# An encoder's neighbourhood attention by pairs of heads: full-height score matmuls, outputs in alternating column halves, queries and keys split straight from PSUM

## The chip, the cores and the metric

The kernel runs on one core of a Trainium2 chip. A core has five engines with queues of their own: TensorE (PE in the profile, its weight loads PEld), VectorE (DVE), ScalarE (ACT), GpSimd (POOL) and SyncE (SP, which here only issues DMAs). The metric is the device time of one execution in microseconds, as the median of several runs. The profile is one further execution, recorded by the hardware profiler; its instructions carry the line numbers of the kernel's file.

## The reference

An encoder of two layers works on 1280 tokens of 1024 channels: 256 of a "prompt" (4 rows of 64) and 1024 of a "sample" (16 rows of 64), each attending only within itself. Layer 0 mixes tokens with a bidirectional RWKV-7 recurrence, layer 1 with a two-dimensional neighbourhood attention of 16 heads of 64 channels; an MLP with squared ReLU follows each. The change touches the attention alone:

```python
def _neighbourhood_attention(h, w_qkv, q_g, k_g, rpb, w_o):
    qkv = (h @ w_qkv).reshape(B, rows, GRID_W, 3, N_HEADS, HEAD_DIM)
    q = _rms_norm(qkv[:, :, :, 0], q_g) * (HEAD_DIM ** -0.5)
    k = _rms_norm(qkv[:, :, :, 1], k_g)
    v = qkv[:, :, :, 2]
    ...
    def row_block(i):
        r0 = jnp.clip(i - kr // 2, 0, rows - kr)
        ...
        s = jnp.einsum('bhcqd,bhrcsd->bhcqrs', q_i, k_s).astype(jnp.float32)
        ...
        s = s + jnp.transpose(bias, (0, 2, 3, 1, 4)).astype(jnp.float32)
        s = jnp.where(col_mask[:, :, None, :], s, -jnp.inf)
        p = jax.nn.softmax(s, axis=(-2, -1)).astype(v_s.dtype)
        o = jnp.einsum('bhcqrs,bhrcsd->bhcqd', p, v_s)
    ...
    return o @ w_o
```

A query sees 8 rows (4 in the prompt) of 16 columns around it. Queries are taken in blocks of 16 columns, and their keys in strips of 32 columns.

## The kernel before

**Data.** Activations lie with channels on the 128 partitions and tokens along the free dimension, 1280 columns in three segments (`SEGS`: 256 of the prompt, 512 and 512 of the sample). Precision beyond one fast pass comes from splitting: a value x becomes a rounded part "hi" of type `float32r` and a rest "lo", and a product of weights w and activations x is three matmuls accumulated in PSUM, w_hi x_hi, w_hi x_lo and w_lo x_hi (`mm3`, lines 93 to 97).

**Blocks.** `attend_all` (line 1637) runs eight blocks m = 0 to 7. A block holds one pair of heads, the 128 channels of its partitions: head e = 0 on partitions 0 to 63 and e = 1 on 64 to 127. While PE works on block m's attention, it also works through the list `work` of block m+1's projections of keys and queries (`qk_proj`, line 1527), a piece at a time; the last block has `output_operands` there, which splits the attention's outputs for the next layer's matmuls and has no matmul. The order of PE's instructions is the program's (`manual_schedule`, line 1644); the order on the other engines is left to the scheduler, so that a PE instruction that waits holds up all that stand behind it on PE.

**Projection.** For keys (`which` = 1), then queries (`which` = 0), and for each segment: 24 matmuls into a PSUM tile `ps` (lines 1553 and 95 to 97), then `evac`. For keys, ACT squares `ps` (L1565) and writes hi to `ks1` (L1577), and DVE writes the rest to `ks0` (L1578). For queries, ACT writes the square and `qf`, the scaled queries with the columns regrouped by blocks of 16 (L1567); ACT copies its halves to `qs0` and `qs1` as hi (L1571), DVE subtracts for the rest `ql` (L1572), and the hi of each head is also copied into the other 64 partitions of its own tile (L1573, ACT or DVE). `stat` sums the squares of each head and token with small matmuls (L1582), `norm` turns the sums into the reciprocal roots of the RMS norms, and `kscale` rebuilds the keys as hi + lo (L1621), scales them (L1622) and splits them again (L1627, L1628). At its end tile `ks`e holds head e's hi in its own 64 partitions and its lo in the other 64.

**Scores.** A score (`score`, lines 1764 to 1769) is two matmuls: 128 rows of `qs`e (hi twice) against `ks`e (hi and lo), which gives hi hi + hi lo, and then 64 rows of `ql` against the 64 rows of `ks`e that hold hi. A sample score has 384 moving columns (12 rows of 32), a prompt score 256.

**Steps.** `attend` (line 1750) builds 20 steps a block, one for each head of 2 prompt and 8 sample query blocks. A step has three parts. A: the score, on DVE the scale and bias (L1802 or L1835) and the maximum (L1775), on ACT the exponential with its sum (L1776), on DVE the reciprocal (L1777) and on POOL the product (L1778). Part two: transposes on PE (L1784) and a copy by ACT (L1786). C: the output matmuls (L1846, L1813), with 64 columns of V as weights, so that head e's output lies in half e of PSUM's partitions; the profile counts two passes for each of these plain float32 matmuls. After the second head, DVE copies both halves out (L1848, L1815). At each step i PE runs A of step i, the transposes of step i-2 and C of step i-3 (one further back in the last block), and after each of the three a share of `work`. The last five pieces of `work` (the last evac, `stat` and `norm` of the queries among them) come after A of the last step. SP's queue carries the weights, the biases (`load_bias`, 8 or 16 DMAs each) and V; POOL's carries the outputs to DRAM (L1746).

Of the kernel before, what the change touches and what calls it, by code (L numbers as in the profile page):

```python
# [5 lines left out]
F32 = mybir.dt.float32  # L6
# [42 lines left out]
class Trunk:  # L49
# [1428 lines left out]
    def attention(self):  # L1478
# [4 lines left out]
        with ExitStack() as ctx:  # L1483
# [8 lines left out]
            self.qke = [pool("qk0"), None]  # L1492
            bp = pool("abp")
# [25 lines left out]
            self.qk = self.qke[1] = pool("aqk", bufs=2)  # L1519
            self.awk = pool("awk", bufs=2)  # L1520
# [4 lines left out]
            self.attend_all(J, work)  # L1525

    def qk_proj(self, m):
# [6 lines left out]
        def load():  # L1534
            for nm in ("ks0", "ks1", "qs0", "qs1", "ql"):
                J[nm] = self.qke[m % 2].tile([P, T], F32R, name=nm, tag=nm, bufs=1)
            for e in range(2):
                J["qs", e], J["ks", e] = J[f"qs{e}"], J[f"ks{e}"]
            J["st"] = self.apn.tile([P, 2, 10, 2], F32, name="nst", tag="nst")
        late = []  # L1540
        for which, wname, g in ((1, "w_nk", self.vec[:, V_KG:V_KG + 1]), (0, "w_nq", self.gq)):
# [3 lines left out]
            for s, (c0, c1) in enumerate(SEGS):  # L1545
# [3 lines left out]
                def mm(k, R=R, which=which, n=n, c0=c0, c1=c1):  # L1549
                    if k == 0:  # L1550
                        R["ps"] = self.apd.tile([P, 512], F32, name="ps", tag="ps")
                    hi, lo = J["w", which]
                    self.mm3(R["ps"][:, :n], hi[:, k * P:(k + 1) * P], lo[:, k * P:(k + 1) * P],
                             act[k][0][:, c0:c1], act[k][1][:, c0:c1], k == 0, k == KT - 1)

                def evac(R=R, which=which, g=g, n=n, c0=c0, c1=c1):
                    ps = R["ps"][:, :n]
                    R["sq"] = self.awk.tile([P, 512], F32, name="sq", tag="sq", bufs=3)
                    sv = R["sq"][:, :n]
                    if which == 0:  # L1560

                        qf = self.awk.tile([P, 512], F32, name="qf", tag="sq", bufs=3)
                        sv = sv.rearrange("p (b r w) -> p r b w", b=4, w=16)
                        ps = ps.rearrange("p (r b w) -> p r b w", b=4, w=16)
                    nc.scalar.activation(sv, ps, AF.Square)  # L1565
                    if which == 0:
                        nc.scalar.activation(qf[:, :n].rearrange("p (b r w) -> p r b w", b=4, w=16), ps, AF.Copy, scale=g)  # L1567
                        for e in range(2):
                            es, eo = slice(64 * e, 64 * e + 64), slice(64 - 64 * e, 128 - 64 * e)
                            qe = J["qs", e][:, c0:c1]  # L1570
                            nc.scalar.copy(qe[es], qf[es, :n])  # L1571
                            nc.vector.tensor_tensor(out=J["ql"][es, c0:c1], in0=qf[es, :n], in1=qe[es].bitcast(F32), op=ALU.subtract)  # L1572
                            (nc.scalar.copy, nc.vector.tensor_copy)[e](qe[eo], qf[es, :n])  # L1573
                    else:

                        kh, kl = J["ks1"][:, c0:c1], J["ks0"][:, c0:c1]
                        nc.scalar.activation(kh, ps, AF.Copy, scale=g)  # L1577
# [354 lines left out]
```

## Time and profile before

| | us |
|---|---|
| median of 3 runs | 4416.08 (4411.3 to 4421.72) |
| the profiled execution | 4410.22 |
| its span, from the first to the last instruction | 4408.4 |
| attention blocks, from the first score to the last one's start | 2809.6 to 3380.0 |

The mean granted TensorE clock was 0.952. In what follows, a row of a timeline gives start, duration, engine, line, operation, tiles (out<-in), the weights' shape and the shape of the moving operand; "x6" says that six instructions in a row are put together. Durations of PE's matmuls are pipelined and overlap. In the windows, each engine has its busy time and number of instructions, and behind them stand the granted clock, the share of DMA and GB/s. A row of grouped instructions gives the total and the mean duration in ns, then the idle time ahead of them and what ended it. In PE's waits the columns are the total, the number and the longest, in us.

### The profile page before, as it was taken

To read this page: it belongs to the slowest core of one execution; us is meant where nothing else is said; L and a number is where in the kernel's file an instruction comes from. 1 tells how busy PE (TensorE), PEld (TensorE's weight loads), DVE (VectorE), ACT (ScalarE), POOL (GpSimd) and SP (SyncE) were. 2 spreads that over 40 slices of the span, in tenths; PEclk is the share of its full clock that TensorE was granted. 3 is DMA by queue.
4 is the path that set the end of the run, shared out by engine and by line. 5 is a ranking of instruction groups with operands and counts; after the bars stand their busy time and mean duration, and the time that the engine had idled before them with its cause. 6 is when DMAs were issued, how large, how long until landed. Compare 5 with 4: busy or idle time off the path is not lost.

```text
span 4408.4 us, 69269 instructions
## 1 busy us (share of the span) xinstructions
PE 4137.4 (94%) x25060; PEld 3408.9 (77%) x25060; DVE 2689.6 (61%) x5322; ACT 1741.1 (39%) x4321; POOL 1610.6 (37%) x1907
## 2 busy tenths in 40 slices
PE   7888989788888879999999999999999999999999
PEld 4664669678778768888888879867776888888888
DVE  7889873577787655655555562355555565555555
ACT  6764442467667743111111133455554311111111
POOL 5446662233433444322222241233344332222222
PEclk8997779899999989999999999999997999999999
DMA  3234455666666442111111115333334211111111
GB/s 120 80 104 177 161 182 145 166 157 154 159 150 157 121 136 78 39 39 39 39 36 37 39 49 164 91 74 65 69 66 128 85 38 35 38 39 39 39 39 58
DMA packets 484152, 400.23 MB, mean 91 GB/s; under 512 B 289153, under 2 KB 392481, under 8 KB 483809
## 3 DMA queue, kind: packets, MB, share of 16 engines
q1 hardware_dynamic: 447584, 328.56, 27.5%
q10 hardware_dynamic: 34416, 61.35, 3.8%
q0 software_dynamic: 1808, 5.90, 0.4%
q8 instruction: 197, 3.23, 0.3%
q14 instruction: 147, 1.20, 0.1%
HBM read 285.66 MB, written 121.24 MB: 92 GB/s over the span
## 4 chain that ended last, share of the span: by engine, by line
PE 67%; DVE 9%; ACT 3%; DMA 2%; issue 2%; POOL 2%; SPq 1%; ACTq 0%; DVEq 0%; POOLq 0%
PE ps L95 17%; PE ps L96 16%; PE ps L97 16%; PE op L1846 2%; DVE tmp L847 2%; DVE q L849 2%; DVE S L1036 1%; PE pt L1784 1%; PE s L1769 1%; PE vps L499 1%; PE vps L500 1%; PE vps L501 1%; PE us L1028 1%; PE aps L807 1%; PE us L1015 1%
## 5 line engine op out<-in xcount | busy, mean ns | idle before, releaser
L1402 DVE TENSOR_TENSOR x<-ps,x 128x256 f32<-128x256 f32 x1488 | 814.7, 595 | 638.1 <-PE ps L97 638.0
L95 PE MATMUL ps<-ah,whi 128*128 128x512 f32 (+1 forms) x2304 | 854.8, 371 | 3.6 <-ACT whi L89 2.9
L96 PE MATMUL ps<-al,whi 128*128 128x512 f32 (+1 forms) x2304 | 827.2, 359 | 2.7 <-POOL al L1292 2.7
L97 PE MATMUL ps<-ah,wlo 128*128 128x512 f32 (+1 forms) x2304 | 824.3, 358 | 1.4 <-POOL wlo L90 1.2
L90 POOL TENSOR_TENSOR wlo<-raw,whi 128x1024 fp32r<-128x1024 f32 (+1 forms) x178 | 391.3, 2198 | 830.1 <-ACT whi L89 829.8
L95 PE MATMUL ps<-hh,whi 128*128 128x512 f32 (+1 forms) x1536 | 547.3, 356 | 14.1 <-DVE x L1402 14.1
L96 PE MATMUL ps<-hl,whi 128*128 128x512 f32 (+1 forms) x1536 | 546.5, 356 | 0.0
L97 PE MATMUL ps<-hh,wlo 128*128 128x512 f32 (+1 forms) x1536 | 545.8, 355 | 0.0
L95 PEld LDWEIGHTS ps<-ah,whi 128*128 128x128 f32 x2304 | 436.2, 189 | 93.3 <-issue 24.0
L97 PEld LDWEIGHTS ps<-ah,wlo 128*128 128x128 f32 x2304 | 435.4, 189 | 71.0 <-POOL wlo L90 2.1
L96 PEld LDWEIGHTS ps<-al,whi 128*128 128x128 f32 x2304 | 436.7, 190 | 63.7 <-POOL al L1292 3.0
L89 ACT CAST whi<-raw 128x1024 fp32r<-128x1024 f32 (+1 forms) x206 | 200.6, 974 | 681.3 <-PE ps L96 647.1
L1381 POOL TENSOR_TENSOR rl<-rl 128x512 f32<-128x512 f32 (+1 forms) x192 | 174.4, 908 | 504.3 <-PE ps L97 462.4
L95 PEld LDWEIGHTS ps<-hh,whi 128*128 128x128 f32 x1536 | 291.2, 190 | 59.4 <-DVE x L1402 17.0
L1023 POOL COPY u<-hv 64x64 f32<-64x64 f32 x640 | 172.5, 270 | 449.9 <-ACT hv L1017 430.3
L97 PEld LDWEIGHTS ps<-hh,wlo 128*128 128x128 f32 x1536 | 291.6, 190 | 41.7
L96 PEld LDWEIGHTS ps<-hl,whi 128*128 128x128 f32 x1536 | 291.0, 189 | 40.6
L1380 ACT ACTIVATE rl<-ps 128x512 f32<-128x512 f32 (+1 forms) x192 | 100.8, 525 | 549.9 <-PE ps L97 549.9
L1383 ACT CAST hh<-rl 128x512 fp32r<-128x512 f32 (+1 forms) x192 | 105.6, 550 | 321.1 <-POOL rl L1381 321.0
L1778 POOL TENSOR_TENSOR s<-s,mx 128x384 f32<-128x384 f32 (+1 forms) x150 | 112.1, 747 | 272.2 <-DVE mx L1777 239.7
L1384 DVE TENSOR_TENSOR hl<-rl,hh 128x512 fp32r<-128x512 f32 (+1 forms) x192 | 119.4, 622 | 151.0 <-ACT hh L1383 150.5
L1036 DVE SCALAR_TENSOR_TENSOR S<-us,dall,sd 64x64 f32<-64x64 f32 x512 | 144.5, 282 | 99.8 <-PE us L1028 91.2
(307 smaller groups left out, 8709.6 us busy)
## 6 DMA issues: line engine op xcount, KB each, us to landing
raw<-in_w_down_dram SPq DMA_DIRECT2D x64, 512.0 KB, 3.5
raw<-in_w_up_dram SPq DMA_DIRECT2D x64, 512.0 KB, 3.4
ar<-ar_d SPq DMA_DIRECT2D x80, 256.0 KB, 3.5
bk<-bk_d SPq DMA_DIRECT2D x80, 256.0 KB, 3.3
ar_d<-ar ACTq DMA_DIRECT2D x32, 512.0 KB, 2.7
bk_d<-bk ACTq DMA_DIRECT2D x32, 512.0 KB, 3.5
bs<-tab SPq DMA_DIRECT2D x128, 96.0 KB, 3.4
v_d<-vt ACTq DMA_DIRECT2D x80, 128.0 KB, 3.8
```

The costliest lines, as they stand in the source:

```text
L89: nc.scalar.copy(hi[:, cs], raw)
L90: lo_eng.tensor_tensor(out=lo[:, cs], in0=raw, in1=hi[:, cs].bitcast(F32), op=ALU.subtract)
L95: mm(ps, sh, mh, start=first, stop=False)
L96: mm(ps, sh, ml, start=False, stop=False)
L97: mm(ps, sl, mh, start=False, stop=last)
L1023: nc.gpsimd.tensor_copy(R["u2"][64 * e:64 * e + 64, 64 * e:64 * e + 64], J["hv"][0:64, cc, 64 * e:64 * e + 64])
L1036: nc.vector.scalar_tensor_tensor(out=S2[es, es], in0=sn[es, es], scalar=D, in1=R["sd"][es, es], op0=ALU.mult, op1=ALU.add)
L1381: nc.gpsimd.tensor_tensor(out=r[:, :n], in0=r[:, :n], in1=r[:, :n], op=ALU.mult)
L1383: nc.scalar.copy(hh[:, :n], r[:, :n])
L1384: nc.vector.tensor_tensor(out=hl[:, :n], in0=r[:, :n], in1=hh[:, :n].bitcast(F32), op=ALU.subtract)
L1402: nc.vector.tensor_tensor(out=xv, in0=ps[:, :n], in1=xv, op=ALU.add)
L1778: nc.gpsimd.tensor_tensor(out=s[:, :nk], in0=s[:, :nk], in1=mx[:, 2:3].to_broadcast([P, nk]), op=ALU.mult)
```

## The change

- **Pairs.** `attend` returns ten pairs instead of twenty steps, each with four parts: A for both heads, transposes of head 0, transposes of head 1, and one C for both. At pair i PE runs A of i, the transposes of head 0 of i-1, C of i-2 and the transposes of head 1 of i-1 (further back in the last block), with a share of `work` after each.
- **Scores.** The rest of the queries gets a tile for each head, `ql0` and `ql1`, with zeros in the other head's 64 partitions (written once by POOL), and the second score matmul takes all 128 rows.
- **Outputs.** C goes through the key tiles and within them through the heads, so that successive output matmuls alternate between the two halves of the columns.
- **Queries.** The projection reads the activations in the order of the query blocks, so that PSUM has them regrouped. ACT writes hi from PSUM, DVE the rest from PSUM, and a DMA on SP copies hi into the other 64 partitions. The square comes after them.
- **Keys.** ACT writes the scaled keys as plain float32 (`kr`); the split before the norm and the addition after it are gone.
- The tag `sq` has two buffers instead of three, and the scratch for POOL's DMAs is 4096 bytes.

```diff
+            self.qlo = [self.low_queries(self.qke[0]), None]
...
+            self.qlo[1] = self.low_queries(self.qk)
...
+    def low_queries(self, pool):
+        ts = [pool.tile([P, T], F32R, name=f"ql{e}", tag=f"ql{e}", bufs=1) for e in range(2)]
+        for e, t in enumerate(ts):
+            self.nc.gpsimd.memset(t[64 - 64 * e:128 - 64 * e].bitcast(F32), 0.0)
+        return ts
...
-                    self.mm3(R["ps"][:, :n], hi[:, k * P:(k + 1) * P], lo[:, k * P:(k + 1) * P],
-                             act[k][0][:, c0:c1], act[k][1][:, c0:c1], k == 0, k == KT - 1)
+                    out, xs = R["ps"][:, :n], [z[:, c0:c1] for z in act[k]]
+                    if which == 0:
+                        out = out.rearrange("p (b r w) -> p b r w", b=4, w=16)
+                        xs = [z.rearrange("p (r b w) -> p b r w", b=4, w=16) for z in xs]
+                    self.mm3(out, hi[:, k * P:(k + 1) * P], lo[:, k * P:(k + 1) * P], *xs, k == 0, k == KT - 1)
...
-                    nc.scalar.activation(sv, ps, AF.Square)
-                    if which == 0:
-                        nc.scalar.activation(qf[:, :n].rearrange("p (b r w) -> p r b w", b=4, w=16), ps, AF.Copy, scale=g)
                         for e in range(2):
                             es, eo = slice(64 * e, 64 * e + 64), slice(64 - 64 * e, 128 - 64 * e)
                             qe = J["qs", e][:, c0:c1]
-                            nc.scalar.copy(qe[es], qf[es, :n])
-                            nc.vector.tensor_tensor(out=J["ql"][es, c0:c1], in0=qf[es, :n], in1=qe[es].bitcast(F32), op=ALU.subtract)
-                            (nc.scalar.copy, nc.vector.tensor_copy)[e](qe[eo], qf[es, :n])
...
+                            nc.scalar.activation(qe[es], ps[es], AF.Copy, scale=g[es])
+                            nc.vector.scalar_tensor_tensor(out=J["ql", e][es, c0:c1], in0=ps[es], scalar=g[es],
+                                                           in1=qe[es].bitcast(F32), op0=ALU.mult, op1=ALU.subtract)
+                            nc.sync.dma_start(qe[eo].bitcast(F32), qe[es].bitcast(F32))
+                    nc.scalar.activation(sv, ps, AF.Square)
+                    if which == 1:
+                        if c0 == 0:
+                            J["kr"] = self.awk.tile([P, T], F32, name="kr", tag="kr", bufs=1)
+                        nc.scalar.activation(J["kr"][:, c0:c1], ps, AF.Copy, scale=g)
...
-                k_ = self.awk.tile([P, 512], F32, name="kf", tag="sq", bufs=3)[:, :c1 - c0]
-                nc.vector.tensor_tensor(out=k_, in0=J["ks1"][:, c0:c1].bitcast(F32), in1=J["ks0"][:, c0:c1].bitcast(F32), op=ALU.add)
+                k_ = J["kr"][:, c0:c1]
...
-                for i, st in enumerate(steps):
-                    pipe.append(st)
-                    for k, lag in enumerate((0, 2, 3) if m < 7 else (0, 3, 4)):
+                for i, pair in enumerate(self.attend(m, J, V)):
+                    pipe.append(pair)
+                    for n, (k, lag) in enumerate(((0, 0), (1, 1), (3, 2), (2, 1)) if m < 7 else ((0, 0), (1, 2), (3, 3), (2, 2))):
                         run(k, lag)
-                        upto = min(len(work) - 5, len(work) * (3 * i + k + 1) // 54) if i < 19 else len(work)
+                        upto = min(len(work) - 5, len(work) * (4 * i + n + 1) // 36) if i < 9 else len(work)
...
-            nc.tensor.matmul(ps, J["ql"][es, qs], k[es], start=False, stop=True)
+            nc.tensor.matmul(ps, J["ql", e][:, qs], k, start=False, stop=True)
...
+        def pair(one, out, nk):
+            Rs = [{}, {}]
+            return (lambda: [one(Rs[e], e) for e in range(2)], lambda: soft2(Rs[0], nk), lambda: soft2(Rs[1], nk), lambda: out(Rs))
...
-                        for t in range(3):
+                    for t in range(3):
+                        for R, es in zip(Rs, heads):
                             nc.tensor.matmul(op[es, :], V[m, 0][:, 4 * cb + rg + t, es], R["st"][:, t * P:(t + 1) * P], start=t == 0, stop=t == 2)
...
-        return prompt[:2] + steps[:4] + prompt[2:] + steps[4:]
+        return prompt[:1] + steps[:2] + prompt[1:] + steps[2:]
...
-    nc = bacc.Bacc("TRN2", target_bir_lowering=False, num_devices=1)
+    nc = bacc.Bacc("TRN2", target_bir_lowering=False, num_devices=1, dynamic_dma_scratch_size=4096)
```

More of the change, by code (lines that the diff above doesn't have):

```diff
@@ new lines, in A @@
+            def A(R, e, j=j):
+                R["ps"] = self.aps.tile([P, 384], F32, name="s", tag="s")
+                score(R["ps"][:, :TP], e, slice(j * P, j * P + P), lambda t: t[:, :TP])
+                R["s"] = scores()
+                v = lambda t: t.rearrange("p (r s) -> p r s", r=4)
+                for u in range(2):
+                    cb, h = 2 * j + u, slice(64 * u, 64 * u + 64)
+                    ss = min(max(cb * 16 - 8, 0), 32)
+                    nc.vector.scalar_tensor_tensor(out=v(R["s"][h, :P]), in0=v(R["ps"][h, :TP])[:, :, ss:ss + 32], scalar=J["rs", 0][h, j, e:e + 1],
+                                                   in1=v(self.bpm[h, e, j]), op0=ALU.mult, op1=ALU.add)
+                soft(R, P)
@@ L1820, in attend @@
+            prompt.append(pair(A, C, P))
         for rg in range(2):
@@ L1855, in run @@
+                steps.append(pair(A, C, 384))
+        return prompt[:1] + steps[:2] + prompt[1:] + steps[2:]
     def run(self, out):
```

114 lines of the change are left out of this document (43 added, 71 removed).

## The prediction

> **What bounds the kernel now.** I read the page first, then the windows of the attention stage, PE's waits there, its groups of instructions, and a timeline of PE alone.
>
> ```profile
> span 4408.4 us, 69269 instructions
> ```
> ```profile
> 3100.00:3200.00 100.00, 100.00 (x563) 72.55 (x562) 56.77 (x147) 50.89 (x132) 38.40 (x46) 1.00 0.36 76
> ...
> 3360.00:3370.00 10.00, 10.00 (x33) 6.36 (x32) 4.37 (x12) 3.16 (x8) 2.92 (x3) 0.50 0.34 103
> ```
> ```profile
> PE ps L95 <- ACT whi L89: 2.9, 1, 2.9
> PE s L1768 <- DVE st L1802: 2.3, 1, 2.3
> ```
>
> The windows give PE, PEld, DVE, ACT, POOL, the granted clock, DMA share and GB/s. Inside the stage PE is busy all the time and the other engines about half of it; PE's two longest waits from 2800 to 3400 us are 2.9 and 2.3 us. So the stage is bound by what PE issues and how fast it can issue it. Its eight blocks (one for each m) have one length:
>
> ```profile
> 3175.29 0.39 PE L1768 MATMUL s<-ks,qs 128*128 128x256 f32 x1
> ...
> 3318.34 0.39 PE L1768 MATMUL s<-ks,qs 128*128 128x256 f32 x1
> ...
> 3318.97 0.38 PE L1768 MATMUL s<-ks,qs 128*128 128x256 f32 x1
> ```
>
> These rows are the first scores of blocks 5 and 7: (3318.34 - 3175.29) / 2 = 71.5 us a block. The last block, which ends near 3389, takes as long without any projection in it, because it runs at a clock of 0.50 (second window row).
>
> Durations of PE rows overlap, so a price is read from start to start:
>
> ```profile
> 3004.41 0.39 PE L97 MATMUL ps<-ah,wlo 128*128 128x512 f32 x1
> 3004.73 0.87 PE L1846 MATMUL op<-st,vs 128*64 128x128 f32 x6
> 3005.53 0.50 PE L95 MATMUL ps<-ah,whi 128*128 128x512 f32 x1
> 3005.86 0.39 PE L96 MATMUL ps<-al,whi 128*128 128x512 f32 x1
> 3006.09 0.39 PE L97 MATMUL ps<-ah,wlo 128*128 128x512 f32 x1
> 3006.33 0.34 PE L1768 MATMUL s<-ks,qs 128*128 128x384 f32 x1
> 3006.59 0.44 PE L1769 MATMUL s<-ks,ql 64*128 64x384 f32 x1
> 3006.97 0.50 PE L95 MATMUL ps<-ah,whi 128*128 128x512 f32 x1
> 3007.31 0.40 PE L96 MATMUL ps<-al,whi 128*128 128x512 f32 x1
> ```
>
> A 512-column pass among others of full shape takes 0.23 us (L96 to L97). Around every pass that uses 64 rows or 64 columns it does not: L97 to op takes 0.32, L95 to L96 after op 0.33, the wide score pass ahead of L1769 0.26, L1769 itself 0.38, and the L95 behind it 0.34. A change of the array's shape costs about 0.1 us on each side, and the next weight load waits for it.
>
> **The change part by part.**
>
> *Scores over 128 rows.* From L1768 at 3006.33 to L96 at 3007.31 are 0.98 us, with one 512-column pass of 0.23 in it: a score costs 0.75. After the change both passes have full shape. A 512-column pass takes 0.23 and a 256-column one 0.12:
>
> ```profile
> 3387.57 1.56 PE L1846 MATMUL op<-st,vs 128*64 128x128 f32 x12
> 3389.06 0.39 PE L95 MATMUL ps<-ah,whi 128*128 128x256 f32 x1
> 3389.28 0.28 PE L96 MATMUL ps<-al,whi 128*128 128x256 f32 x1
> 3389.40 0.28 PE L97 MATMUL ps<-ah,wlo 128*128 128x256 f32 x1
> ```
>
> so 384 columns take about 0.18, a score 0.36, and 0.39 us are saved. A prompt score takes 0.63 (3318.34 to 3318.97) against 2 x 0.12, again 0.39. Twenty scores a block: 7.8 us.
>
> *Outputs in alternating column halves.* Six passes of one head cost 3004.41 to 3005.86 = 1.45, less two 512-column passes = 0.98 us, of which 0.80 is from the first pass to the L95. The pair now costs 1.97. Afterwards its twelve passes stand in one group, with the heads alternating. There are two ends. If the halves work one after the other, the group is the x12 row: 1.49 to the L95 and 0.18 for the two sides, 1.67, so 0.30 is saved. If they work side by side, the pair costs what one head costs, and 0.98 is saved. The nearest rows for that choice:
>
> ```profile
> 1203.49 0.44 PE L909 MATMUL qps<-qq,yt 32*32 32x32 f32 x16
> 1203.87 0.33 PE L949 MATMUL lps<-cst,bk 128*128 128x128 f32 x1
> ```
> ```profile
> L1846 PEld LDWEIGHTS op<-st,vs x768: 132/137/231, 2828.5 to 3388.7; 128*64 128x64 f32 x192
> ```
>
> At L909 sixteen passes alternate between two separate quarters of the array in 0.38 us with both changes of shape, some 0.2 of which are the sides: 0.01 to 0.02 us a pass. Six 128-column passes in 0.80, less 0.15 for the sides, are 0.11 a pass, so 32 columns alone would need 0.027. The two quarters therefore overlap. They differ in rows too, though; no row shows halves that share all rows. I take the full overlap, and keep the serial end for the range. Eight sample pairs save 7.8 a block. A prompt pair (four short passes a head) is about half of that, 2 x 0.5: 8.8 us a block in all.
>
> The Trainium skill, page "TensorE: Matmul & The Clock Gate", section "Part 3: Packing small matmuls — row/col tiling", says that a weight load runs beside running matmuls only if its row group differs; column halves share their row groups, so by that rule the serial end would hold. The trace differs for one half: loads of 137 ns and passes of 110 ns, six of each one after the other, would be 1.5 us, and they take 0.80.
>
> *Queries and keys straight from PSUM.*
>
> ```profile
> L1565 ACT ACTIVATE sq<-ps 128x512 f32<-128x512 f32 x30 | 17.8, 593 | 14.7 <-PE ps L97 14.7
> L1567 ACT ACTIVATE qf<-ps,gq 128x512 f32<-128x512 f32 x16 | 11.0, 686 | 0.2
> L1571 ACT CAST qs<-qf 64x512 fp32r<-64x512 f32 x32 | 19.8, 618 | 0.4
> L1572 DVE TENSOR_TENSOR ql<-qf,qs 64x512 fp32r<-64x512 f32 x32 | 28.8, 899 | 1.6 <-ACT qs L1571 0.9
> L1578 DVE SCALAR_TENSOR_TENSOR ks<-ps,vec,ks 128x512 fp32r<-128x512 f32 x14 | 10.5, 747 | 6.3 <-ACT ks L1577 6.3
> ```
>
> For a 512-column query piece ACT had 0.59 + 0.69 + three casts of 0.62 = 3.1 us and has two scaled copies (0.69) and the square, 2.0. DVE had two subtractions of 0.90 and one cast, and has two at about 0.75. For a key piece DVE loses the 0.75 of L1578 and the addition of L1621. With ACT and DVE at 51 and 57% none of this is on the path: zero. It would cost its own length only if ACT came to bind, and ACT gets shorter. It matters as margin, because the same softmax work now falls into shorter blocks: from 57 and 51% of 71.5 us, less these, I estimate some 37 us for DVE and 34 for ACT, of 55.
>
> *Six more transfers a block on SP* carry half the rows of the queries.
>
> ```profile
> raw<-in_w_nq_dram SPq DMA_DIRECT2D x5, 256.0 KB, 4.5
> ```
>
> They have at most half of that size, so I estimate under 4.5 us. The first pair of a block reads columns of segment 0, the second of segment 1, which were projected a whole segment (24 x 0.23 = 5.6 us and the attention between) earlier; segment 2 is read six pairs later. SP issues them behind bias and weight loads, which wait too; these in turn are queued behind the new ones by under half a microsecond each. I cost it at nothing, with that slack as its cover; if it fails, one wait of 4.5 us a block, 32 us.
>
> *Queries projected with blocks in order.* The same passes and columns, but the moving operand is read in runs of 16 elements. The nearest row is a score, read in runs of 32:
>
> ```profile
> L96 PE MATMUL ps<-al,whi 128*128 128x512 f32 x242 | 95.8, 396 | 0.0
> L96 PE MATMUL ps<-al,whi 128*128 128x256 f32 x127 | 37.5, 295 | 0.0
> ...
> L1768 PE MATMUL s<-ks,qs 128*128 128x384 f32 x128 | 50.8, 397 | 3.3 <-DVE st L1802 2.3 <-DVE s L1802 1.0
> ...
> L1768 PE MATMUL s<-ks,qs 128*128 128x256 f32 x32 | 11.2, 351 | 0.0
> ```
>
> Contiguous columns: (396 - 295) / 256 = 0.39 ns each. From 256 contiguous to 384 in runs: 46 / 128 = 0.36. Runs cost nothing, and I take zero for runs of 16 as well. Memsets, the third buffer less and the smaller scratch for POOL's transfers: 1 us together, once.
>
> *Steps of pairs instead of heads.*
>
> ```profile
> 3181.61 0.62 DVE L1835 SCALAR_TENSOR_TENSOR s<-s,rs,bs 128x384 f32<-128x384 f32 x1 [0.74 <-PE s L1769]
> ...
> 3185.74 0.82 POOL L1778 TENSOR_TENSOR s<-s,mx 128x384 f32<-128x384 f32 x1 [0.84 <-DVE mx L1777]
> ```
>
> This is one head's softmax, from the first operation on DVE to the product on POOL: 4.95 us to its end, with DVE's other head in between. From a pair's scores to its first transposes PE will have about one pair of other work, 55 / 10 = 5.5 us, and to the second head's two transposes more. That holds inside a block, narrowly. At a block's end it is tighter: after the last projection piece PE has an output group, transposes and two scores (some 2 us) before the query statistics, which need the square, now the third operation on ACT (0.69 + 0.69 + 0.59 and the handover: 2.5). The last pair's transposes follow its scores after about 3 us of PE work, against those 4.95. I take 3 us of new waits for each of seven blocks, 21 us; from the same sums 0 to 6 a block.
>
> *The last block* has no projection. At clock 0.50:
>
> ```profile
> 3371.57 1.47 PE op L1846 x6
> 3373.04 0.62 PE s L1768
> ...
> 3374.27 0.83 PE pt L1784 x3
> 3375.10 1.47 PE op L1846 x6
> ```
>
> A head takes 3.53, a pair 7.06. Afterwards: four score passes at twice 0.18, 1.4; transposes 1.6; one group 1.5; 4.5 us. Ten pairs would save some 25; DVE, ACT and POOL also split 21 pieces of the operands there, so I take 22.
>
> **Sum.** 7 x (7.8 + 8.8) = 116 saved, 21 given back at the block ends, 1 for the memsets, 22 from the last block: 116 us. The profiled execution took 4410.2 us (span 4408.4): 4294. The median of the runs, 4416.1, is 6 above it: **4300 us**.
>
> **The rivals.**
>
> *The halves work one after the other.* 1.97 becomes 1.67: 0.3 x 8 + 0.5 = 2.9 a block, not 8.8. That gives back 7 x 5.9 = 41, and about 5 in the last block: 4346. For it speaks that no row shows halves with common rows side by side; against it, L909.
>
> *The softmax chain takes PE's place.* If every pair waits 0.6 us more for POOL's product, 70 pairs give back 42 us: 4342. For it: the chain of two heads is in order on DVE. Against: 5.5 us stand against 4.95, part of which was queueing, and DVE has a third of the block free.
>
> *Slower: the query projection reads short runs slowly.* A block has 1280 columns x 24 passes of it, 24 x 2.5 x 0.23 = 13.8 us; 8 blocks, 110 us. At half rate this eats the whole gain (4410), and from a factor of a little over 2 the kernel is slower; at a quarter of the rate it costs 331: 4631. Against it stand the 0.36 ns a column above.
>
> *Nothing comes of it*: scores stay at 0.75, because the drain belongs to the wide moving operand. Against: L97 to L1768 takes 0.24.
>
> **Chances.** Forecast 0.63; serial halves 0.16; softmax chain 0.13; slow runs 0.05 (0.02 near no change, 0.03 slower); nothing 0.03. A measurement of this kernel tells about 0.2% from no change. Faster 0.92, same 0.04, slower 0.04. The range reaches from no waits at the block ends with a last block 14 us better still (4265) to the serial halves and the chain with some more waits (4352).
>
> **What would show it.** Right: L1768 and L1769 0.18 apart, twelve output passes in some 0.8 us, blocks of 55 to 58 us, no PE wait over 3 us. Wrong: output passes 0.11 apart, query L95 to L96 over 0.25, PE waiting on POOL's product or on a transfer into qs at each block's start.

## The result, and the profile after

| | before | after |
|---|---|---|
| median of the runs, us | 4416.38 (4411.3 to 4421.72) | 4372.15 (4367.69 to 4377.02) |
| ratio | | 0.9900, 95% interval 0.9883 to 0.9917 |
| span of the profiled execution | 4408.4 | 4367.5 |
| first score of block 0 | 2809.6 | 2814.5 |
| blocks 0 to 6, mean length | 72.7 | 69.1 |
| block 7, to the first matmul behind it | 70.7 | 50.0 |

The kernel became 44 us faster, 1.0%. The forecast was 116 us, 4300, and the range ended at 4352: the time lies outside it. Three of its steps can be read directly in the trace of after, and they came out as written. First the scores and outputs (timeline; start, duration, engine, line, operation, tiles, shapes; in brackets an idle time and who ended it):

```profile
3151.18 0.88 PE L1846 MATMUL op<-st,vs 128*64 128x128 f32 x12
...
3151.99 0.55 PE L1788 MATMUL pt<-cst,s 128*128 128x128 f32 x3
...
3152.55 0.34 PE L1773 MATMUL s<-ks,ql 128*128 128x384 f32 x1
...
3152.73 0.34 PE L1772 MATMUL s<-ks,qs 128*128 128x384 f32 x1
...
3152.91 0.34 PE L1773 MATMUL s<-ks,ql 128*128 128x384 f32 x1
```

The score passes start 0.18 us apart (3152.55, .73, .91), and the twelve output passes of a pair take 0.81 (3151.18 to 3151.99), as long as the six of one head did before. The projection of queries, with its short runs, and that of keys, with contiguous columns, stand in the same timeline:

```profile
3135.05 0.40 PE L95 MATMUL ps<-ah,whi 128*128 128x512 f32 x1
3135.29 0.40 PE L96 MATMUL ps<-al,whi 128*128 128x512 f32 x1
3135.52 0.39 PE L97 MATMUL ps<-ah,wlo 128*128 128x512 f32 x1
...
3173.49 0.40 PE L96 MATMUL ps<-al,whi 128*128 128x512 f32 x1
3173.73 0.40 PE L97 MATMUL ps<-ah,wlo 128*128 128x512 f32 x1
3173.96 0.40 PE L95 MATMUL ps<-ah,whi 128*128 128x512 f32 x1
```

The first three belong to queries, the last three to keys. Both are 0.24 and 0.23 apart.

What the sum missed is in the windows. Here are blocks 0 to 6 as one window, before first (length, busy time and instructions of PE, PEld, DVE, ACT, POOL, granted clock, DMA share, GB/s):

```profile
2809.60:3318.30 508.70, 503.72 (x2763) 365.16 (x2763) 287.29 (x721) 261.92 (x664) 197.20 (x230) 0.98 0.30 66
```

And after:

```profile
2814.50:3298.30 483.80, 427.64 (x2758) 354.15 (x2758) 232.97 (x660) 240.73 (x622) 194.19 (x230) 0.91 0.36 79
```

Such a row splits in three. **Idle** is the length less PE's busy time: 5.0 us before, 56.2 after. The **clock's loss** is the length times what is missing to a clock of 1: 0.02 x 508.7 = 10 before, 0.09 x 483.8 = 44 after (the clock is rounded, so each is good to 2.5 us). The rest is PE's **work** at full clock: 493 before, 384 after, 70.5 and 54.9 us a block. So PE's work shrank by 15.6 us a block, and 51 us of new idle time and 33 us of lower clock took most of it back. PE's waits in the same window say who the idle time belongs to (total, number, longest):

```profile
PE nst L1587 <- ACT sq L1579: 37.9, 21, 3.6
PE ps L95 <- ACT whi L89: 13.2, 4, 3.3
PE ps L97 <- POOL wlo L90: 5.1, 4, 1.3
```

These three are all of the 56.2. Two thirds is the statistics' wait for the square, 21 waits in seven blocks: one for each segment of queries. The longest kind looks like this in the timeline of ACT, DVE and PE, at the end of block 4:

```profile
3150.85 0.40 PE L97 MATMUL ps<-ah,wlo 128*128 128x512 f32 x1
...
3151.61 0.68 ACT L1575 ACTIVATE qs<-ps,gq 64x512 fp32r<-64x512 f32 x1
...
3152.32 0.74 DVE L1576 SCALAR_TENSOR_TENSOR ql<-ps,gq,qs 64x512 fp32r<-64x512 f32 x1
...
3152.62 0.48 ACT L1790 COPY st<-pt 128x384 f32<-128x384 f32 x1 [0.34 <-PE pt L1788]
...
3153.13 0.68 ACT L1575 ACTIVATE qs<-ps,gq 64x512 fp32r<-64x512 f32 x1
...
3154.70 0.61 ACT L1780 ACTIVATE s<-s,mx 128x384 f32<-128x384 f32 x1 [0.89 <-DVE mx L1779]
...
3155.10 0.76 DVE L1576 SCALAR_TENSOR_TENSOR ql<-ps,gq,qs 64x512 fp32r<-64x512 f32 x1
...
3155.32 0.60 ACT L1780 ACTIVATE s<-s,mx 128x384 f32<-128x384 f32 x1
...
3156.03 0.60 ACT L1579 ACTIVATE sq<-ps 128x512 f32<-128x512 f32 x1
...
3156.68 1.87 PE L1587 MATMUL nst<-cst,sq 128*128 128x2 f32 x8 [3.42 <-ACT sq L1579]
```

The PSUM tile was complete at 3151.25. The square is not merely third on ACT, behind the two scaled copies. On ACT's queue a copy of transposes stands between these, and the last pair's two exponentials stand ahead of the square; ACT idles 0.89 us until DVE has the maximum for them. DVE is in the way as well: its second subtraction (L1576) reads the same tile `ps`, stands behind the last pair's work on DVE and ends only at 3155.86, 0.17 us before the square starts. A shorter tile of the same projection, segment 0, shows the two engines taking turns at `ps`:

```profile
3127.14 0.45 ACT L1575 ACTIVATE qs<-ps,gq 64x256 fp32r<-64x256 f32 x1
...
3127.63 0.47 DVE L1576 SCALAR_TENSOR_TENSOR ql<-ps,gq,qs 64x256 fp32r<-64x256 f32 x1 [0.20 <-ACT qs L1575]
...
3128.14 0.47 ACT L1575 ACTIVATE qs<-ps,gq 64x256 fp32r<-64x256 f32 x1 [0.18 <-DVE ql L1576]
...
3128.64 0.49 DVE L1576 SCALAR_TENSOR_TENSOR ql<-ps,gq,qs 64x256 fp32r<-64x256 f32 x1 [0.54 <-ACT qs L1575]
...
3129.16 0.38 ACT L1579 ACTIVATE sq<-ps 128x256 f32<-128x256 f32 x1 [0.56 <-DVE ql L1576]
```

Each of these starts when the other engine's has ended, and so it is everywhere in the attention blocks: between 2800 and 3300 us no read of `ps` by ACT overlaps one by DVE in any trace of this case (155 reads in after). What makes them take turns the traces do not say. The square is therefore the fifth operation of a chain on two engines; for 512 columns the rows above add up to 0.68 + 0.74 + 0.68 + 0.76 + 0.60 = 3.5 us without anything between. Here it ends at 3156.63, 5.4 us after its data was there, and PE stood still for 3.42 of them. The eight small matmuls then take 1.87 us; without a wait ahead of them they take 0.95 (the same timeline, some 44 us earlier):

```profile
3112.15 0.95 PE L1587 MATMUL nst<-cst,sq 128*128 128x2 f32 x8
```

The granted clock is 0.50 over the first of these rows (3156.6 to 3158.5) and 1.00 over the second. That is the half clock which follows the wait.

### The profile page after: what moved, and what is told of

It reads as the page before. It is cut to its first block, busy times and chain, and to the rows that moved or that the text cites. A ratio compares the mean times of both kernels' runs of the same rounds, so it can differ in the third digit from the quotient of the medians.

```text
span 4367.5 us, 69360 instructions
## 1 busy us (share of the span) xinstructions
PE 4024.1 (92%) x25060; PEld 3378.6 (77%) x25060; DVE 2632.5 (60%) x5250; ACT 1715.0 (39%) x4273; POOL 1610.4 (37%) x1911
## 4 chain that ended last, share of the span: by engine, by line
PE 64%; DVE 10%; ACT 4%; DMA 2%; issue 2%; POOL 2%; SPq 1%; ACTq 0%; DVEq 0%; POOLq 0%
PE ps L95 16%; PE ps L96 16%; PE ps L97 16%; DVE tmp L847 2%; DVE q L849 1%; DVE S L1036 1%; PE vps L499 1%; PE vps L500 1%; PE vps L501 1%; PE us L1028 1%; PE pt L1788 1%; PE op L1846 1%; PE aps L807 1%; PE nst L1587 1%; PE us L1015 1%
## 5 line engine op out<-in xcount | busy, mean ns | idle before, releaser
L95 PE MATMUL ps<-ah,whi 128*128 128x512 f32 (+1 forms) x2304 | 850.4, 369 | 13.2 <-ACT whi L89 13.2
```

The lines of the kernel that those rows point to most:

```text
L95: mm(ps, sh, mh, start=first, stop=False)
```

## The experiments

The theory: the change's three PE terms are right, and what is missing went into the waits for the square and the half clock behind them. The rivals: a PE term is smaller than it looks; the steps by pairs or the transfers cost it; the half clock has a cause of its own. Each run's ratio is to the kernel before on the same chip.

| run | median, us | ratio (95%) |
|---|---|---|
| square first | 4318.11 | 0.9778 (0.9760 to 0.9795) |
| heads in turn | 4377.17 | 0.9908 (0.9894 to 0.9923) |
| low part over 64 rows | 4449.79 | 1.0073 (1.0058 to 1.0088) |
| square first, evac a piece earlier | 4319.85 | 0.9778 (0.9762 to 0.9795) |
| square first, bias after the weights | 4332.81 | 0.9814 (0.9792 to 0.9837) |
| square first, pieces spread to the end | 4315.76 | 0.9770 (0.9754 to 0.9786) |
| before + full-row scores | 4338.20 | 0.9825 (0.9810 to 0.9839) |
| before + outputs of both heads together | 4351.54 | 0.9854 (0.9840 to 0.9869) |
| before + both | 4301.36 | 0.9740 (0.9723 to 0.9756) |
| the same, new evac, square first | 4299.90 | 0.9740 (0.9721 to 0.9759) |
| the same, new evac, square last | 4324.27 | 0.9790 (0.9776 to 0.9805) |
| after, waits filled with work | 4352.38 | 0.9865 (0.9848 to 0.9881) |

**1. The square first.** One line of the changed kernel is moved:

```diff
                     sv = R["sq"][:, :n]
+                    nc.scalar.activation(sv, ps, AF.Square)
                     if which == 0:
...
-                    nc.scalar.activation(sv, ps, AF.Square)
                     if which == 1:
```

> The changed kernel with the query's square moved ahead of the two scaled copies on ACT, nothing else. Theory (PE waits at the query statistics L1587 for the square, 5.7 us a block, and each wait is followed by a stretch at half clock): the 43.8 us of PE waiting for the square fall under 6 us, the half-clock stretches in blocks 0 to 6 fall from about 100 us to under 40, blocks take 57 to 60 us instead of 69, and the time falls from 4372 to about 4300 (4285 to 4320). Rival (the chain of the softmax by pairs now paces the blocks, and the waits at the statistics only stand where others would): the waits turn up at the transposes L1788, blocks stay over 66 us, and the time stays over 4355.

4318.11 us, 54 faster than the change as it stands. The window of blocks 0 to 6, and PE's waits in it:

```profile
2805.00:3240.40 435.40, 399.29 (x2758) 333.83 (x2758) 230.12 (x654) 234.40 (x617) 192.16 (x227) 0.96 0.39 87
```
```profile
PE ps L95 <- ACT whi L89: 13.6, 3, 5.1
PE pt L1788 <- ACT rs L1162: 9.8, 6, 1.8
PE pt L1788 <- ACT st L1790: 9.2, 6, 3.0
```

The wait for the square is gone from the list. The clock's loss falls from 44 to 17 us, PE's work stays (54.6 us a block), and idle falls only from 56 to 36: once the square is early, the transposes at a block's end wait for ACT (19.0 us in the last two rows) where after had none in its blocks. A wait removed uncovers the next one, but a shorter one. The theory's place is right, and the time is in its range; a block comes to 62.2 us, not 57 to 60.

**2. The heads in turn.** The two loops of the output matmuls are exchanged in the changed kernel (the prompt's likewise), so one head's passes all come before the other's:

```diff
-                    for t in range(3):
-                        for R, es in zip(Rs, heads):
+                    for R, es in zip(Rs, heads):
+                        for t in range(3):
```

> The changed kernel with the output matmuls of head 0 all before those of head 1, as before the change; still one group for the pair. Theory (the two column halves work side by side, and this was worth 0.67 us a sample pair): twelve passes take 1.49 us instead of 0.81, seven blocks get 5.9 us longer each, and the time rises by about 40 us (25 to 50; less than 41 where a wait absorbs it) to about 4410. Rival (PE's issue no longer bounds the blocks, the waits do): under 10 us.

4377.17: 5 us slower than the change, not 40. The timeline of this kernel's PE shows why:

```profile
3003.48 1.14 PE L1846 MATMUL op<-st,vs 128*64 128x128 f32 x12
3004.55 0.50 PE L95 MATMUL ps<-ah,whi 128*128 128x512 f32 x1
```

The group takes 1.07 us, between the 0.81 of alternating halves and the 1.49 of the row of before which the prediction took for the serial end. So two halves overlap also where the heads are not alternated, wherever they meet. This expectation missed: most of the gain lies in having both heads in one group. Alternating them adds 0.26 us a pair, 15 us over the 56 sample pairs of blocks 0 to 6. The time shows 5 of them, but not because waits took up the rest, as the rival had it. These are blocks 0 to 6:

```profile
2821.57:3306.36 484.79, 429.63 (x2758) 358.38 (x2758) 234.16 (x660) 241.02 (x622) 194.52 (x230) 0.94 0.37 80
```

Work is (429.63 - 0.06 x 484.79)/7 = 57.2 us a block, 2.3 more than after, and idle is 55, as in after. It is the clock's loss that fell, from 44 to 29 us; why, with the same waits, is not shown. So the time of this run doesn't measure the alternation.

**3. The low part over 64 rows.** In the changed kernel, the second score matmul again uses the 64 rows that hold something:

```diff
-            nc.tensor.matmul(ps, J["ql", e][:, qs], k, start=False, stop=True)
+            es = slice(64 * e, 64 * e + 64)
+            nc.tensor.matmul(ps, J["ql", e][es, qs], k[es], start=False, stop=True)
```

> The changed kernel with the second score matmul over 64 rows again. Theory (a pass over 64 rows costs a change of shape on both sides, 0.39 us a score, and PE bounds the blocks outside the waits): 140 scores in blocks 0 to 6 cost 54 us more, the last block some more, so the time rises by 40 to 60 us to about 4420. Rival (absorbed in the waits): under 20 us.

4449.79: 78 us slower than the change, slower even than before. The window of its blocks 0 to 6:

```profile
2815.50:3366.50 551.00, 497.98 (x2757) 368.93 (x2758) 239.45 (x660) 241.14 (x622) 194.31 (x230) 0.88 0.32 70
```

Work is (497.98 - 0.12 x 551)/7 = 61.7 us a block, 6.8 more than after: 0.34 us for each of 20 scores. Idle is 53, as in after, and the clock's loss 66, 22 more. The full rows are worth what the prediction said, nearly (0.39 there): 48 of the 78 us over seven blocks. Of the rest, 22 are lower clock and 8 a longer last block (58.0 for 50.0); so the time lies above the expected 40 to 60.

**4. The evac a piece earlier.** Square first, and the last evac leaves the block's tail:

```diff
-                        upto = min(len(work) - 5, len(work) * (4 * i + n + 1) // 36) if i < 9 else len(work)
+                        upto = min(len(work) - 4, len(work) * (4 * i + n + 1) // 36) if i < 9 else len(work)
```

> As a1, and the last query piece's evacuation is issued with the fill, ahead of the last pair's scores (four instead of five pieces are kept back). Theory: with the square first, ACT takes it up as soon as the projection ends in either order, so within 8 us of a1. Rival (the order of issue puts the square behind the exponentials of the last pair): a1 keeps a wait of over 2 us at each block's end and a4 is 15 to 40 us faster than a1.

4319.85, as the first experiment. The rest of the waiting isn't decided by where the evac stands in PE's program.

**5. The bias after the weights.** Square first, and one of three bias loads is issued a block later, to let the weights' loads pass:

```diff
-                        if i in (3, 5, 9):
-                            self.load_bias(m + 1, (2, 0, 1)[i // 4])
+                        if i in (3, 5):
+                            self.load_bias(m + 1, (2, 0)[i // 4])
...
                         self.load_v(V, m, 0)
+                        self.load_bias(m, 1)
```

> a1 with the eight bias loads that stood at a block's end moved behind the next block's weight loads on SP. Theory (PE's waits of up to 5 us for the rounded weights at L95 come from the weight load standing behind eight bias loads of 0.45 us each): these waits fall from 13.6 us to under 4, with the half-clock stretch behind each the time falls 8 to 25 us below a1's 4318. Rival (the waits only move to the transposes of the last pair): within 6 us of a1.

4332.81: not faster, as expected, but if anything slower (4324 to 4345 against 4313 to 4329 in the first experiment; the ranges overlap). In the stage (2800 to 3350) PE's waits for weights grew:

```profile
PE ps L95 <- ACT whi L89: 17.8, 6, 3.2
...
PE ps L97 <- POOL wlo L90: 7.7, 11, 1.4
```

They were 13.6 and 2.1 with the square first alone. The bias loads at the block's end aren't what delays the weights; what does was not found.

**6. The pieces spread to the end.** Square first, and the list `work` reaches to the block's last slot, so the last pair has matmuls beside it:

```diff
+                        if m < 7:
+                            upto = min(len(work) - 5, len(work) * (4 * i + n + 1) // 40) if i < 9 or n < 3 else len(work)
...
```

> a1 with the projection's pieces spread over all forty slots of a block instead of the first thirty-four, so that PE has projection work beside the last pairs' softmax, and the last statistics come after the last slot. Theory (the remaining waits at the transposes, 30 us, stand at the block's end, where PE has no projection left): the waits at L1788 fall under 18 us, most of them in the last block, and the time falls by 8 to 25 us below a1. Rival (the later statistics delay the next block's first pair as much): within 6 us of a1 or slower.

4315.76, within the scatter of the first experiment. In the stage, the transposes' waits fell from 30.2 us to 18.6, while the scores' waits for DVE and the statistics' for the square rose from 2.2 to 11.4: moved, not removed.

**7 and 8. One part of the change each, in the kernel before.** First the full rows alone (with `low_queries` and its zeroed halves), then the outputs of both heads in one alternating group, with steps by single heads:

```diff
-            nc.tensor.matmul(ps, J["ql"][es, qs], k[es], start=False, stop=True)
+            nc.tensor.matmul(ps, J["ql", e][:, qs], k, start=False, stop=True)
```
```diff
-                        if e == 0:
+                        if e == 1:
...
-                        for t in range(3):
-                            nc.tensor.matmul(op[es, :], V[m, 0][:, 4 * cb + rg + t, es], R["st"][:, t * P:(t + 1) * P], start=t == 0, stop=t == 2)
+                            for t in range(3):
+                                for R, es in zip(Rs, heads):
+                                    nc.tensor.matmul(op[es, :], V[m, 0][:, 4 * cb + rg + t, es], R["st"][:, t * P:(t + 1) * P], start=t == 0, stop=t == 2)
```

> The kernel before with only the scores changed: a tile of query rests for each head with zeros in the other 64 rows, and the second score matmul over all 128 rows. Steps, outputs, projection and evacuation as before. Theory (a score costs 0.75 us and becomes 0.36, PE bounds every block): blocks fall from 71.5 to 63.7 us, the last block by some 10, the time by 65 us (50 to 80) to about 4352. Rival (the term of 0.39 us a score was too large, and this is where the forecast failed): less than 5 us a block, less than 40 us in all.

> The kernel before with only the outputs changed: the output matmuls of both heads in one group after the second head's transposes, the heads alternating. Theory (the pair's group costs 0.98 us instead of 1.97): blocks fall from 71.5 to about 62.7 us, the last block by about 10, the time by 70 us (55 to 85) to about 4347. Rival (the halves follow one another, 0.3 us a pair): 2.9 us a block, 20 to 30 us in all.

4338.20 and 4351.54: 79 and 65 us faster than before. Blocks 0 to 6 of the first:

```profile
2813.50:3275.70 462.20, 450.33 (x2764) 363.82 (x2763) 286.73 (x721) 260.75 (x664) 196.47 (x230) 0.99 0.34 73
```

And of the second:

```profile
2808.40:3270.30 461.90, 449.81 (x2759) 332.61 (x2758) 283.53 (x718) 260.06 (x664) 201.38 (x230) 0.97 0.32 73
```

Idle is 12 us in each. Work is 63.7 and 62.3 us a block: 6.8 and 8.2 less than before (7.8 and 8.8 forecast). Either part alone gives more than the whole change. What takes the gain away is in the change's other parts, or in having both at once, which the next run tries.

**9. Both together**, still with the old evac and single heads:

> The kernel before with full-row scores (b1) and paired outputs (b2) together, steps by single heads and the old evacuation kept. Theory (both terms are PE's own time and add): 78 and 65 us faster alone, so 143 together, 4274 us (4260 to 4295), blocks of 57 to 59 us. Rival (at such block lengths another engine's chain paces the blocks, as the 62 us of a1 suggest): over 4300.

4301.36, 115 us faster than before, the best version here with the next one, and 28 short of the sum of the two, so the expected 4274 was missed, and the rival's mark, over 4300, just met. Blocks 0 to 6:

```profile
2803.10:3228.00 424.90, 398.81 (x2758) 330.84 (x2758) 282.08 (x718) 260.50 (x663) 201.44 (x230) 0.98 0.34 79
```

Work is 55.8 us a block, 14.7 less than before: PE's terms add up. Idle is 26.1, 21 more than before, where the two parts alone had 7 more each. And the last block doesn't get shorter twice. It was 70.8 long at a clock of 0.57 before, and is 45.9 with full rows alone, 59.7 with the outputs alone, and 51.0 with both (windows, in that order):

```profile
3318.30:3389.06 70.76, 66.00 (x230) 41.48 (x229) 39.47 (x93) 33.49 (x91) 32.42 (x37) 0.57 0.37 110
```
```profile
3275.70:3321.60 45.90, 36.83 (x230) 27.25 (x229) 37.96 (x93) 33.54 (x92) 32.90 (x37) 0.93 0.49 144
```
```profile
3270.30:3330.00 59.70, 50.83 (x237) 31.45 (x234) 38.46 (x96) 33.74 (x92) 31.75 (x36) 0.57 0.44 129
```
```profile
3228.00:3279.00 51.00, 36.49 (x238) 25.67 (x236) 38.45 (x96) 33.42 (x93) 31.18 (x36) 0.73 0.44 130
```

With both parts PE is busy 36.5 of 51.0 us there: it no longer binds that block, so saving more on PE can bring little. Of the 28 us, 16 (24.9 + 11.1 - 19.8) are this. In the profiled executions the first block also starts 6.5 us earlier than before, which is not explained; that the rest lies in the new idle time fits, but the medians can't be divided so finely.

**10 and 11. The new evac with steps by single heads**, with the square first, and then last as in the change:

```diff
                     sv = R["sq"][:, :n]
-                    nc.scalar.activation(sv, ps, AF.Square)
                     if which == 0:
...
+                    nc.scalar.activation(sv, ps, AF.Square)
                     if which == 1:
```

> b3 with the whole of the changed projection and evacuation, the square first as in a1; so it is a1 with steps by single heads. Theory (what a1 still waits for at its blocks' ends comes from the steps by pairs): within 10 us of b3, and 25 us or more below a1's 4318. Rival (it comes from the new evacuation and its transfers on SP): within 10 us of a1.

> b5 with the square behind the copies, as in the change. Theory (the square's place on ACT makes PE wait at the statistics; with steps by heads PE has more work between the last piece and its statistics): waits at L1587 of 1 to 3 us a block, 10 to 30 us slower than b5. Rivals: as with the pairs, 45 us or more slower (the place of the square alone decides), or under 5 us (only the pairs' order made it late).

4299.90 and 4324.27. With the square first, queries split straight from PSUM, the strided projection and the transfers on SP cost nothing and bring nothing (4301.36 with the old evac). With the square last, 24 us are lost, against 54 with steps by pairs. The wait is the same with a smaller size, as PE's waits in blocks 0 to 6 of the last one show, and at its block ends the square waits for DVE's second subtraction, as in this row of ACT:

```profile
PE nst L1587 <- ACT sq L1579: 20.4, 21, 2.8
```
```profile
3248.27 0.60 ACT L1579 ACTIVATE sq<-ps 128x512 f32<-128x512 f32 x1 [0.61 <-DVE ql L1576]
```

The longest wait is 2.8 us, not 3.6. In after two exponentials of a pair stand ahead of the square as well; that these make the difference fits, but was not tried by itself. With the square first, steps by pairs look 18 us slower than steps by heads (4318.11 against 4299.90, where 25 or more were expected), but the two profiled executions differ by 1.4 us only (4313.6 and 4312.2), and both kernels scatter by some 16 to 21 us: that price isn't settled.

**12. The waits filled.** The changed kernel, square last, with matmuls that nobody needs ahead of the query statistics:

```diff
...
+                    if which == 0 and c0:
+                        for _ in range(9 if c0 == SEGS[1][0] else 18):
+                            nc.tensor.matmul(J["fill"][:, 64:448], J["w", 0][0][:, :P], act[0][0][:, :384], start=True, stop=True)
                     for b in range(n // P):
```

> The changed kernel, with the square left last. PE gets superfluous matmuls (384 columns, 0.18 us each) ahead of the query statistics: 9 of them (1.6 us) for segment 1, 18 (3.2 us) for segment 2, so the time in which it waits there for the square (about 1.7 and 3.7 us in the changed kernel) is filled with work instead. Their result is used by nothing. Theory: the stretches at half clock follow from those waits. They were 91 us in blocks 0 to 6 of the changed kernel and cost about half their length more; without the waits they fall to about 35 us, the wait at the statistics from 43.8 to about 10 us, and the time falls by 20 to 30 us, to 4342 to 4352, although PE does no useful work in the filled time. Rival: the half clock has another cause (the load over a longer stretch, or the last block's), and the waits cost only their own length: the half clock stays near 90 us and the time within 8 of the changed kernel, 4364 to 4380. If above 4380, the filling itself is late somewhere or costs more than the wait did.

4352.38: 20 us faster than the change, by giving PE more to do. Timeline, window of blocks 0 to 6, and PE's waits in it:

```profile
3134.86 3.34 PE L1589 MATMUL nst<-ah,whi 128*128 128x384 f32 x18
3138.58 1.05 PE L1591 MATMUL nst<-cst,sq 128*128 128x2 f32 x8 [0.38 <-ACT sq L1580]
```
```profile
2809.70:3274.70 465.00, 434.49 (x2948) 363.95 (x2947) 231.27 (x659) 239.06 (x621) 193.63 (x229) 0.97 0.37 82
```
```profile
PE nst L1591 <- ACT sq L1580: 5.8, 12, 0.7
```

The wait of 3.4 us became 18 passes of 0.18 and a wait of 0.38, and the eight matmuls behind it take 1.05 us, not 1.87. The fill is 7 x 27 = 189 passes, some 34 us, and with the 5.8 us that are still waited it takes about as long as the 37.9 of waiting did. The statistics come no earlier, then; what changed is the clock's loss, 44 to 14 us (a clock of 0.97 for 0.91). The other waits grew by 6, and the blocks are 18.8 us shorter together. That most of the half clock of after follows from these waits is shown.

What is not shown is a fixed price. For 53 to 56 us of idle time the clock's loss was 44 us in after, 29 with the heads in turn and 66 with 64 rows; for 36 it was 17 with the square first. Nor are waits the only cause: from 2946.98 to 2953.81 of experiment 8 the granted clock was 0.50 with PE busy all the time, and its longest wait from 2930 on was 0.6 us.

## Why the prediction was wrong, point by point

- **What binds.** Right for the kernel before: PE. Its work a block fell from 70.5 to 54.9 us. The prediction's own sum before the waits was 71.5 - 16.6 = 54.9. That the two agree so closely owes something to chance: the 71.5 held about 1 us that isn't work, and the PE terms make 15.6, not 16.6.
- **Scores.** The mechanism right, the term a little large: 0.18 us apart, as said; 6.8 us a block measured twice (experiments 3 and 7) for 7.8.
- **Outputs.** Right in size, 8.2 us a block for 8.8, and in the choice of full overlap: 0.81 us a group. The rival of serial halves is out, and with it the rule of the Trainium skill that was weighed there (page "TensorE: Matmul & The Clock Gate", "Part 3: Packing small matmuls — row/col tiling"), by which loads overlap with running matmuls only for other row groups: these halves share all rows. But the alternation itself carried less than was thought: heads in turn take 1.07 us, 0.26 more. The x12 row of before, from which the serial end was taken, wasn't a price of that order. In it the second head's passes had to wait for ACT's copy of their operand, which ended at 3388.21, 0.64 after the first pass:

```profile
3387.73 0.48 ACT L1786 COPY st<-pt 128x384 f32<-128x384 f32 x1 [1.08 <-PE pt L1784]
```

- **Queries straight from PSUM, the transfers on SP, strided projection.** Costed at nothing, and nothing they cost (4299.90 against 4301.36), while the square is first. PE didn't wait for a transfer into `qs` in any of the listed waits.
- **The step that failed** is "I take 3 us of new waits for each of seven blocks, 21 us; from the same sums 0 to 6 a block". Measured are 8.0 us of idle time a block (56.2/7) and 6.2 of lower clock (43.5/7), 14.2 together, of which before had 2.2 (0.7 and 1.5): 12 new ones in place of 3. With the 54.9 of work they make the block's 69.1. Three things were wrong in it. It priced the square as "the third operation on ACT (0.69 + 0.69 + 0.59 and the handover: 2.5)", as if ACT took the three in one go. In the trace the square is the fifth operation of a chain in which ACT and DVE take turns at `ps`, 3.5 us at the least, and with the other work that both engines put between it took 5.4. It looked only at block ends, but the statistics of every segment wait: 21 waits, not 7. And it gave the wait its own length as its price: the lower clock cost nearly as much again. Experiment 1 shows that these waits hang on the square's place, experiment 12 that the clock's loss hangs on the waits. What held the square up, the turns with DVE or the exponentials ahead of it, is read from the rows; no run took one away and left the other. Of the prediction's own signs of being right, blocks of 55 to 58 us and no wait of PE over 3 us did not come: they are 69.1 and 3.6.
- **Weights.** Not in the sum: 18.3 us of waits for whi and wlo (13.2 + 5.1) where before had 4.0 (2.9 + 1.1). Perhaps the same transfers come later relative to PE in shorter blocks; why they are late was not found (experiment 5 missed).
- **The softmax chain.** In after its waits don't show, since PE waits elsewhere first. With the square first the transposes, which stand behind that chain, wait 19.0 us for ACT. The rival's place is right, as second in line, and its 42 us are too many.
- **The last block.** -20.7 us (70.7 to 50.0) for -22. The size fits, the reason less so: PE, forecast to be the bound there, is busy for 32.7 of 50.0 us, as this window of after shows, and the granted clock, taken as 0.50 for the whole block, is 0.78.

```profile
3298.26:3348.23 49.97, 32.72 (x236) 24.12 (x234) 37.52 (x87) 32.53 (x88) 32.49 (x35) 0.78 0.43 138
```

Its length went from 45.9 to 59.7 us between the runs above, and the granted clock in it from 0.93 with the full rows alone to 0.57 with the outputs alone, which the prediction didn't foresee; agreement to a few us is luck.

## What to carry to other kernels

When an edit shortens the work of an engine that was always busy, its sum is the easy half: list every point where that engine takes something from another, and for each the time between the data being there and the consumer's turn, on the other engine's real queue with all that may stand in it. Where two engines read one result, look in a trace whether they take turns, and add up the whole chain. Among several operations that read one result, the one whose consumer sits on the bound engine goes first. And price a wait on TensorE above its length, because the clock can fall behind it: in these runs by about half as much again (17 us for 36 in experiment 1) to more than as much again (66 for 53 in experiment 3). Where a wait can't be removed, look whether the bound engine can be given work in it.

## What the hardware showed that was not expected

- A wait of 1.56 us on PE was already followed by a lower clock (timeline of after; the three transposes took 0.49 before it and 0.88 behind it):

```profile
2928.29 0.49 PE L1788 MATMUL pt<-cst,s 128*128 128x128 f32 x3
...
2933.22 1.11 PE L1587 MATMUL nst<-cst,sq 128*128 128x2 f32 x8 [1.56 <-ACT sq L1579]
2934.20 0.88 PE L1788 MATMUL pt<-cst,s 128*128 128x128 f32 x3
```

  The Trainium skill, page "TensorE: Matmul & The Clock Gate", section "HAM oscillation — how this bites in real kernels", names gaps of more than about 3.4 us as what brings the lower clock. The rows here put it lower. But a wait of that length is not always followed by it: in experiment 1 PE waited 1.61 us until 2863.82, and the granted clock was 1.00 from there to 2867.80.
- ACT and DVE never read one PSUM tile of the projection at the same time: 155 reads of `ps` between 2800 and 3300 us of after, none overlapping between the engines.
- Superfluous matmuls in PE's idle time made the kernel 20 us faster, by the clock alone.
- Twelve output passes whose column halves share all 128 rows take 0.81 us alternating and 1.07 one head after the other; six of one half alone had taken 0.80.
